# Two raw weight sums placed together on VectorE in the down-projection groups of a two-layer decoder trunk

## The chip, the cores and the metric

The kernel runs on one core of a Trainium2 chip. The metric is the device time of one execution in microseconds. A time before or after is the median over several runs; beside it stands one execution that was taken with the hardware profiler, and the rows of the trace come from that one.

## The reference

Two layers work on 512 tokens of width 1024, in float32. `ffn*_wd` is 2816 x 1024, `w_out` 1024 x 1024:

```python
for l in range(DEPTH):
    x = x + 0.5 * swiglu(rms_norm(x, ffn1_norm[l]), ffn1_wg[l], ffn1_wu[l], ffn1_wd[l])
    h = rms_norm(x, mix_norm[l])
    z = h @ w_in[l]                      # q, k, v and the three inputs of the convolution
    attn_out = sliding_window_attention(q, k, v, attn_sink[l])
    conv_out = short_conv(...)
    x = x + jnp.concatenate([attn_out, conv_out], axis=-1) @ w_out[l]
    x = x + 0.5 * swiglu(rms_norm(x, ffn2_norm[l]), ffn2_wg[l], ffn2_wu[l], ffn2_wd[l])
return rms_norm(x, final_norm)
# swiglu(h, g, u, d) = (silu(h @ g) * (h @ u)) @ d
```

## The kernel before

**Products in two parts.** Every operand of a matrix product is kept as a pair: a rounded high part and the rest. A weight tile is loaded as `raw` (128 x 1024 float32). ScalarE casts it to `wh` and VectorE subtracts, which gives `wl = raw - wh` (`split`, L226). TensorE multiplies three times: high by high, high by low, low by high.

**Seven products instead of eight.** Most of the large products are done in Strassen's manner, on two by two blocks. The weights then take seven forms (`FORMS`: a11, a12, s2, s3, s1, a22, s4) in this order. s1 and s3 are made while loading: SP's queue loads one block and POOL's queue adds another into the same tile (`need_raw`, L221). s2 is a11 + s1, summed on VectorE in place of a11 (L265). s4 is a12 + s2, which POOL's queue adds from tile to tile (L295). The products' accumulators are named x, y and w; `CHAINS` gives the order in which TensorE takes them. The activation forms are b11, b21, t2, t3, t1, t4 and b22, and they are split in the same way (`ft1h`, `ft1l` and so on).

**Groups.** The stages of a feed-forward network are written out by hand in `FIRST`, `INNER` and `LAST`. An entry ("s", b) is a group of down-projection products over 1024 of the 2816 inner columns. `plan` orders its weights with `seven`, and marks them "share": each form comes in two halves h = 0 and 1, so there are 14 weight tiles to a group. There are seven such groups: two in each of the first three networks, one in the last. In the first network the weights stand still and the activations stream in matmuls of 256 columns (`stand`, L815); in the others the matmuls have 512 columns (`stream`, L830). The output projection `w_out` uses the same forms, with `state["late"]` set.

**Order.** `take_split` hands TensorE its next weight pair and calls `need_split` for the pair two further on (`SPLIT_AHEAD` = 2). `need_split` calls `need_raw`, which issues loads at least four tiles ahead (`LOAD_AHEAD`). There are 8 places for raw tiles and 3 each for `wh` and `wl`. Apart from the opening and the end, a scheduler arranges each engine's instructions when the kernel is built, by dependences and priorities; `tc.issue_after(i)` makes what is inside come after the instruction i in this order. `state["rest"]` is the last split's subtraction. For a group "s" the sum of each half is issued after the last split's subtraction: so the first sum comes after a12's last subtraction, and the second sum after the subtraction of the first half of s2.

Of the kernel before, what the change touches and what calls it, by code (L numbers as in the profile page):

```python
# [75 lines left out]
def trunk_kernel(  # L76
# [23 lines left out]
    nc = tc.nc  # L100
# [94 lines left out]
    raw_of, split_of = {}, {}  # L195
    roomy = set()
    state = {"raw": 0, "split": 0, "group": 0, "late": None}
# [13 lines left out]
    def need_raw(u):  # L211

        while state["raw"] <= min(u, len(units) - 1):
            n = state["raw"]
            _, _, kc, _, wide = units[n][0]
            name, shape = f"raw_{n}", (P, kc, wide)
            r = form(name, F32, shape) if n in roomy else stock(name, shape=shape)
            if n >= OPEN:
                load(r, n, 0, kc)
            for more in units[n][1:]:  # L220
                nc.gpsimd.dma_start(out=r, in_=rows_of(*more), accum_op=ALU.add)  # L221
            raw_of[n] = r
            state["raw"] += 1

    def split(hi, lo, raw, eng=nc.vector):
        return nc.scalar.copy(hi, raw), eng.tensor_sub(lo, raw, f32(hi))  # L226

    def split_far(hi, lo, raw):

        nc.scalar.activation(lo, raw, AF.Copy, scale=-1.0)  # L230
        nc.scalar.copy(hi, raw)
        return nc.gpsimd.dma_start(out=f32(lo), in_=raw, accum_op=ALU.add)

    def need_split(g):
        while state["split"] <= min(g, len(order) - 1):
            n = state["split"]
            u, what = order[n]
            far = what == "far"
            if what in (None, "far"):
                need_raw(u if far else u + LOAD_AHEAD)  # L240
                raw = raw_of.pop(u)
            elif isinstance(what, tuple) and what[0] == "end":

                _, what, h = what
                at = {"a11": 2, "s2": 2, "s3": 3, "s1": 3, "a12": 4, "a22": 5, "s4": 5}[what]
                need_raw(u + 3 * at + h + LOAD_AHEAD)
                raws = {name: u + 3 * i + h for i, name in enumerate(END_LOADS)}
                if what == "s2":
                    with tc.issue_after(state["rest"]):
                        nc.vector.tensor_add(raw_of[raws["a11"]], raw_of[raws["a11"]], raw_of[raws["s1"]])  # L250
                raw = raw_of[raws["a11" if what in ("s2", "s4") else what]]
            elif isinstance(what, tuple):

                what, h, how = what
                far = how == "far"
                last = {"a11": 0, "a12": 4, "s2": 2, "s3": 6, "s1": 2, "a22": 8, "s4": 4}[what]
                need_raw(u + h if far else u + max(last, 4) + h + LOAD_AHEAD)
                a11, s1, a12, s3, a22 = (raw_of.get(u + 2 * i + h) for i in range(5))
                if what == "s2":

                    late = state["late"] if h else None
                    if not state["late"] and how == "share":
                        late = state["rest"]
                    with tc.issue_after(late) if late else nullcontext():
                        nc.vector.tensor_add(a11, a11, s1)  # L265
                raw = {"a11": a11, "a12": a12, "s2": a11, "s3": s3, "s1": s1, "a22": a22, "s4": a12}[what]
            else:

                need_raw(u + 4 + LOAD_AHEAD)
                a11, a12, s1, s3, a22 = (raw_of.get(u + i) for i in range(5))  # L270
                if what == "s2":
                    nc.vector.tensor_add(a11, a11, s1)
                if what == "s4":
                    nc.vector.tensor_add(a11, a11, a12)
                raw = {"a11": a11, "a12": a12, "s2": a11, "s3": s3, "s1": s1, "a22": a22, "s4": a11}[what]
                if what == FORMS[-1]:
                    for i in range(5):
                        del raw_of[u + i]
            shape = list(raw.shape)
            hi = wpool.tile(shape, F32R, tag="wh", bufs=3, name=f"wh_{n}")  # L280
            lo = wpool.tile(shape, F32R, tag="wl", bufs=3, name=f"wl_{n}")
            if far:
                sent = split_far(hi, lo, raw)
            else:
                state["cast"], state["rest"] = (i.ins for i in split(hi, lo, raw))
            if isinstance(order[n][1], tuple) and order[n][1][0] == "end":
                if what == "a12":
                    nc.gpsimd.dma_start(out=raw_of[raws["a11"]], in_=raw, accum_op=ALU.add)
                if what in ("s3", "s1", "a12", "a22"):
                    del raw_of[raws[what]]  # L290
                if what == "s4":
                    del raw_of[raws["a11"]]
            elif isinstance(order[n][1], tuple):
                if what == "s3" and how == "share":
                    nc.gpsimd.dma_start(out=a12, in_=a11, accum_op=ALU.add)  # L295
                elif what == "s3":
                    nc.vector.tensor_add(a12, a12, a11)
                done = {"s3": (0, 3), "s1": (1,), "a22": (4,), "s4": (2,)}.get(what, ())
                for i in done:
                    del raw_of[u + 2 * i + h]  # L300
            split_of[n] = (hi, lo)
            state["split"] += 1
            if far:

                with tc.issue_after(sent.ins):
                    need_raw(u + LOAD_AHEAD + (4 + h if isinstance(order[n][1], tuple) else 0))

    def take_split(ahead=SPLIT_AHEAD):
        n = state["group"]
        state["group"] += 1  # L310
        need_split(n + ahead)
        return n, *split_of.pop(n)
# [406 lines left out]
    with tc.manual_schedule(engines={pe, act, dve}):  # L719
# [41 lines left out]
        state["split"] = state["group"] = OPEN  # L761
        squares(2)
        need_split(OPEN)
        squares(3)

# [748 lines left out]
    def mix(l, norm, after):  # L1514
# [153 lines left out]
        def go_on():  # L1668

            nonlocal step  # L1670
            last = attend(step)
            step += 1
            with tc.issue_after(last.ins) if last else nullcontext():
                need_split(state["group"] - 1 + SPLIT_AHEAD)
# [89 lines left out]
```

## Time and profile before

| | us |
|---|---|
| median of 3 runs | 1645.42 |
| lowest and highest run | 1642.57, 1646.46 |
| profiled execution | 1643.27 |
| its span in the trace | 1641.5 |
| TensorE, matmul | 1631.8 busy |
| VectorE | 1376.5 busy |
| ScalarE | 1115.8 busy |
| GpSimd | 212.2 busy |

The granted TensorE clock was 0.999. A row of the timeline gives the start in us, the length in us, the engine, the line of the kernel, the operation, the tiles written and read, and a count; in brackets stands the idle time of the engine just before, and what ended it. The starts of two matmuls tell more than their lengths, since matmuls are pipelined. L815 and L830 are the products of `stand` and `stream`, L226 is `split`, L265 the sums, L221 and L295 the adding loads and copies of POOL's queue.

### The profile page before, as it was taken

The numbers are of one execution on the slowest core, as the hardware profiler recorded it, in microseconds if no ns is written. First come the engines' busy times: TensorE is split into PE (matmuls) and PEld (weight loads), VectorE is DVE, ScalarE is ACT, GpSimd is POOL, SyncE is SP. The second block draws the span as 40 slices with busy tenths as digits, with TensorE's granted clock in tenths as the row PEclk, the third lists the DMA queues.
The fourth block names the chain that finished last, engine by engine and source line by source line (L and its number), as shares of the span: only waits on it lengthen the run. The fifth ranks groups of instructions, "written<-read, shape, count | busy, mean of one in ns | idle before, by whom it ended". The sixth has DMA issues, their size and how long they took to land.

```text
span 1641.5 us, 22019 instructions
## 1 busy us (share of the span) xinstructions
PE 1631.8 (99%) x8060; PEld 1378.9 (84%) x8060; DVE 1376.5 (84%) x1812; ACT 1115.8 (68%) x1461; POOL 212.2 (13%) x188
## 2 busy tenths in 40 slices
PE   9999999999999999999999999999999999999998
PEld 7888889988898888888888888888888988888887
DVE  7987779987899977798998777989788998777997
ACT  6447776466567577777865777788565766777665
POOL 0011111100221011111011111110012111111121
PEclk9999999999999999999999999999999999999999
DMA  8379897741397689999966999999125967999992
GB/s 257 86 197 213 220 246 187 173 131 52 103 225 184 178 214 217 218 209 242 233 145 169 228 214 226 209 239 215 51 65 136 233 146 187 222 222 225 244 252 72
DMA packets 281504, 307.15 MB, mean 187 GB/s; under 512 B 98028, under 2 KB 166708, under 8 KB 281396
## 3 DMA queue, kind: packets, MB, share of 16 engines
q1 hardware_dynamic: 240804, 223.29, 47.2%
q0 software_dynamic: 39872, 81.80, 29.2%
q8 instruction: 63, 1.03, 0.2%
q10 hardware_dynamic: 720, 0.66, 0.1%
q14 instruction: 45, 0.37, 0.1%
HBM read 262.71 MB, written 2.10 MB: 161 GB/s over the span
## 4 chain that ended last, share of the span: by engine, by line
PE 93%; DVE 4%; ACT 1%; DMA 1%; issue 1%; SPq 0%; ACTq 0%; DVEq 0%
PE x L830 25%; PE y L830 13%; PE acc L324 7%; PE acc L325 7%; PE acc L327 7%; PE w L830 6%; PE x_s L830 5%; PE y_s L830 3%; PE x_m L815 3%; PE x_s L815 2%; PE w_s L830 2%; PE y_s L815 1%; PE y_m L815 1%; DVE wl L226 1%; PE acc L710 1%; PE x_e L830 1%
## 5 line engine op out<-in xcount | busy, mean ns | idle before, releaser
L226 ACT CAST wh<-raw 128x1024 fp32r<-128x1024 f32 (+1 forms) x491 | 511.1, 1044 | 363.0 <-PE x L830 91.9
L226 DVE TENSOR_TENSOR wl<-raw,wh 128x1024 fp32r<-128x1024 f32 (+1 forms) x491 | 594.8, 1218 | 175.3 <-ACT wh L226 174.0
L325 PE MATMUL acc<-xl,wh 128*128 128x512 f32 x424 | 165.7, 391 | 0.3 <-DVE xl L480 0.3
L324 PE MATMUL acc<-xh,wh 128*128 128x512 f32 x424 | 165.8, 392 | 0.0
L327 PE MATMUL acc<-xh,wl 128*128 128x512 f32 x416 | 162.3, 390 | 0.0
L221 POOL DMA_DIRECT2D raw<-in_ffn_wu_dram x39 | 49.0, 1256 | 394.6 <-DMA raw<-in_ffn_wu_dram 261.1
L325 PEld LDWEIGHTS acc<-xl,wh 128*128 128x128 f32 x424 | 79.7, 188 | 16.9 <-DVE xl L480 1.1
L324 PEld LDWEIGHTS acc<-xh,wh 128*128 128x128 f32 x424 | 79.8, 188 | 15.7
L327 PEld LDWEIGHTS acc<-xh,wl 128*128 128x128 f32 x416 | 78.1, 188 | 16.2
L221 POOL DMA_DIRECT2D raw<-in_ffn_wg_dram x39 | 48.1, 1258 | 228.6 <-DMA raw<-in_ffn_wu_dram 96.0
L221 POOL DMA_DIRECT2D raw<-in_ffn_wd_dram x34 | 41.0, 1209 | 249.0 <-DMA raw<-in_ffn_wd_dram 102.9
L265 DVE TENSOR_TENSOR raw<-raw,raw 128x1024 f32<-128x1024 f32 x56 | 68.0, 1219 | 3.9 <-DMA raw<-in_ffn_wu_dram 2.1
L1161 ACT COPY raw_a<-turned 128x1024 uint16<-128x1024 uint16 x48 | 63.1, 1355 | 0.0
L830 PE MATMUL w<-wh,fb21h 128*128 128x512 f32 x152 | 59.2, 390 | 0.0
L830 PE MATMUL x<-wh,ft2h 128*128 128x512 f32 x152 | 59.2, 390 | 0.0
L830 PE MATMUL y<-wh,ft3h 128*128 128x512 f32 x152 | 59.2, 390 | 0.0
L830 PE MATMUL x<-wl,ft1h 128*128 128x512 f32 x152 | 59.2, 389 | 0.0
L830 PE MATMUL x<-wh,ft1h 128*128 128x512 f32 x152 | 59.1, 389 | 0.0
L830 PE MATMUL w<-wh,fb21l 128*128 128x512 f32 x152 | 59.1, 389 | 0.0
L830 PE MATMUL x<-wl,ft2h 128*128 128x512 f32 x152 | 59.1, 389 | 0.0
L830 PE MATMUL w<-wl,fb21h 128*128 128x512 f32 x152 | 59.1, 389 | 0.0
L830 PE MATMUL x<-wh,ft2l 128*128 128x512 f32 x152 | 59.1, 389 | 0.0
(607 smaller groups left out, 4627.2 us busy)
## 6 DMA issues: line engine op xcount, KB each, us to landing
raw<-in_ffn_wu_dram SPq DMA_DIRECT2D x126, 512.0 KB, 5.4
raw<-in_ffn_wd_dram SPq DMA_DIRECT2D x105, 512.0 KB, 5.8
raw<-in_ffn_wg_dram SPq DMA_DIRECT2D x86, 512.0 KB, 5.3
raw<-in_ffn_wu_dram POOLq DMA_DIRECT2D x39, 512.0 KB, 9.1
raw<-in_ffn_wg_dram POOLq DMA_DIRECT2D x39, 512.0 KB, 6.6
raw<-in_w_in_dram SPq DMA_DIRECT2D x36, 512.0 KB, 3.8
raw<-in_ffn_wd_dram POOLq DMA_DIRECT2D x34, 512.0 KB, 9.5
raw<-raw POOLq DMA_DIRECT2D x21, 512.0 KB, 6.8
```

The costliest lines, as they stand in the source:

```text
L221: nc.gpsimd.dma_start(out=r, in_=rows_of(*more), accum_op=ALU.add)
L226: return nc.scalar.copy(hi, raw), eng.tensor_sub(lo, raw, f32(hi))
L265: nc.vector.tensor_add(a11, a11, s1)
L324: nc.tensor.matmul(acc, hi[:, k, :], rhs[k][0], start=k == first, stop=False)
L325: nc.tensor.matmul(acc, hi[:, k, :], rhs[k][1], start=False, stop=False)
L327: nc.tensor.matmul(acc, lo[:, k, :], rhs[k][0], start=False, stop=k == last)
L710: nc.tensor.matmul(opening[n], (lo if part == "w" else hi)[:, k, :], xl if part == "x" else xh, start=n not in begun, stop=k == KC - 1 and ...
L815: nc.tensor.matmul(accs[c // 2][:, c % 2, :], w[:, k, cols], x_[:, 2 * h + k, :], start=start and c % 2 == 0 and h + k + i == 0, stop=h + ...
L830: nc.tensor.matmul(accs[u], x_[:, 2 * h + k, tok], w[:, k, :], start=start and h + k + i == 0, stop=h + k == 2 and i == 2, skip_group_chec ...
L1161: nc.scalar.copy(words(raws[self.b][:, c, :]), self.to[:, :, c, :])
```

## The change

For the groups marked "share" outside the output projection, the sum of s2 is now made for both halves at the half h = 0: two sums, one after the other, both issued after the last split's subtraction, which is then that of a12's second half. At h = 1 nothing is summed. The branch for all other users of these forms keeps its sum and, in the output projection, its `state["late"]`. The number of instructions is the same on every engine.

```diff
-                if what == "s2":
-
-                    late = state["late"] if h else None
-                    if not state["late"] and how == "share":
-                        late = state["rest"]
-                    with tc.issue_after(late) if late else nullcontext():
+                if what == "s2" and how == "share" and not state["late"]:
+
+
+                    if h == 0:
+                        with tc.issue_after(state["rest"]):
+                            for k in range(2):
+                                to = raw_of[u + k]
+                                nc.vector.tensor_add(to, to, raw_of[u + 2 + k])
+                elif what == "s2":
+                    with tc.issue_after(state["late"]) if h and state["late"] else nullcontext():
                         nc.vector.tensor_add(a11, a11, s1)
```

In the order that the scheduler then writes, the two sums stand next to each other or with one subtraction or one update between them, ahead of the first `wl` of s2. In groups 1, 2, 4 and 6 TensorE's matmuls around s2 also change places among themselves. In the last group two loads of SP trade places with two of the closing stage.

## The prediction

> **What bounds the kernel now.** I read the page first: the busy times, the chain that ended last, and the group of the sums that the change moves.
>
> ```profile
> PE 1631.8 (99%) x8060; PEld 1378.9 (84%) x8060; DVE 1376.5 (84%) x1812; ACT 1115.8 (68%) x1461; POOL 212.2 (13%) x188
> PE 93%; DVE 4%; ACT 1%; DMA 1%; issue 1%; SPq 0%; ACTq 0%; DVEq 0%
> L265 DVE TENSOR_TENSOR raw<-raw,raw 128x1024 f32<-128x1024 f32 x56 | 68.0, 1219 | 3.9 <-DMA raw<-in_ffn_wu_dram 2.1
> ```
>
> TensorE (PE) is busy for 1631.8 of 1641.5 us and holds 93% of the chain. VectorE (DVE) is busy for 1376.5 us. So an edit on VectorE changes the time only where TensorE is seen to wait for it. A sum takes 1.22 us; 14 of the 56 are touched, two in each of seven groups "s", here numbered in order of time. No sum is added or removed: both are put before the first split, and the second no longer waits for it. Next I read the timeline of each group, VectorE, ScalarE (ACT) and TensorE in turn. Group 1:
>
> ```profile
> 258.41 1.22 DVE L265 TENSOR_TENSOR raw<-raw,raw 128x1024 f32<-128x1024 f32 x1
> 259.61 1.22 DVE L226 TENSOR_TENSOR ft1l_s<-raw_a,ft1h_s 128x1024 fp32r<-128x1024 f32 x1
> 260.82 1.23 DVE L226 TENSOR_TENSOR wl<-raw,wh 128x1024 fp32r<-128x1024 f32 x1
> 261.96 1.22 DVE L265 TENSOR_TENSOR raw<-raw,raw 128x1024 f32<-128x1024 f32 x1
> 264.37 1.23 DVE L226 TENSOR_TENSOR wl<-raw,wh 128x1024 fp32r<-128x1024 f32 x1 [1.19 <-ACT wh L226]
> ...
> 259.74 1.05 ACT L226 CAST wh<-raw 128x1024 fp32r<-128x1024 f32 x1 [0.16 <-DVE raw L265]
> 263.29 1.05 ACT L226 CAST wh<-raw 128x1024 fp32r<-128x1024 f32 x1 [2.50 <-DVE raw L265]
> ...
> 261.46 0.28 PE L815 MATMUL x_s<-ft2h_s,wh 128*128 128x256 f32 x1
> 261.58 0.28 PE L815 MATMUL x_s<-ft2l_s,wh 128*128 128x256 f32 x1
> 262.10 0.39 PE L815 MATMUL x_s<-ft2h_s,wl 128*128 128x256 f32 x1 [0.24 <-DVE wl L226]
> 265.34 0.39 PE L815 MATMUL y_s<-ft3h_s,wh 128*128 128x256 f32 x1
> 268.20 0.28 PE L815 MATMUL y_s<-ft3h_s,wl 128*128 128x256 f32 x1
> ```
>
> The old chain stands here: sum, cast on ScalarE, subtraction (wl), second sum, cast, subtraction, and VectorE is idle for 1.19 us before the last. TensorE's matmuls of 256 columns start 0.12 apart (261.46 to 261.58). So 262.10 is 0.40 late: it waits for the first wl, which ends at 260.82 + 1.23 = 262.05. And 265.34 is 0.26 late (the matmul before it starts at 264.96).
>
> Group 4 has the later form, with matmuls of 512 columns:
>
> ```profile
> 771.38 1.21 DVE L265 TENSOR_TENSOR raw<-raw,raw 128x1024 f32<-128x1024 f32 x1
> 772.51 1.22 DVE L226 TENSOR_TENSOR ft1l_s<-raw_a,ft1h_s 128x1024 fp32r<-128x1024 f32 x1
> 773.78 1.23 DVE L226 TENSOR_TENSOR wl<-raw,wh 128x1024 fp32r<-128x1024 f32 x1
> 774.93 1.22 DVE L265 TENSOR_TENSOR raw<-raw,raw 128x1024 f32<-128x1024 f32 x1
> 777.34 1.23 DVE L226 TENSOR_TENSOR wl<-raw,wh 128x1024 fp32r<-128x1024 f32 x1 [1.19 <-ACT wh L226]
> 780.70 1.23 DVE L226 TENSOR_TENSOR wl<-raw,wh 128x1024 fp32r<-128x1024 f32 x1 [0.94 <-ACT wh L226]
> ...
> 776.25 1.05 ACT L226 CAST wh<-raw 128x1024 fp32r<-128x1024 f32 x1 [2.50 <-DVE raw L265]
> ...
> 775.00 0.39 PE L830 MATMUL x_s<-wh,ft2h_s 128*128 128x512 f32 x1
> 778.17 0.39 PE L830 MATMUL x_s<-wh,ft2h_s 128*128 128x512 f32 x1
> 778.62 0.50 PE L830 MATMUL x_s<-wl,ft2h_s 128*128 128x512 f32 x1
> 778.95 0.39 PE L830 MATMUL x_s<-wh,ft2h_s 128*128 128x512 f32 x1
> 781.53 0.40 PE L830 MATMUL y_s<-wh,ft3l_s 128*128 128x512 f32 x1
> 781.99 0.50 PE L830 MATMUL y_s<-wl,ft3h_s 128*128 128x512 f32 x1
> ```
>
> 775.00 to 778.17 are 14 starts, so a pitch of 0.226. 778.62 comes 0.22 late for the second wl, and the start after it (778.95) is 0.10 slow as well: a stall of 0.33 us. 781.99 is late by 0.23 for the wl of 780.70, with the same tail: again 0.33. Group 6 is group 4's twin in the next layer and shows the pair in its row of 1101.77, below. The rest have cover, that is, the first wl is done well before TensorE first reads it:
>
> ```profile
> 1101.33 0.39 PE L830 MATMUL x_s<-wh,ft2h_s 128*128 128x512 f32 x1
> 1101.77 0.50 PE L830 MATMUL x_s<-wl,ft2h_s 128*128 128x512 f32 x1
> ...
> 312.04 1.22 DVE L226 TENSOR_TENSOR wl<-raw,wh 128x1024 fp32r<-128x1024 f32 x1
> 313.82 0.28 PE L815 MATMUL x_s<-ft2h_s,wl 128*128 128x256 f32 x1
> ...
> 734.19 1.23 DVE L226 TENSOR_TENSOR wl<-raw,wh 128x1024 fp32r<-128x1024 f32 x1 [1.36 <-ACT wh L226]
> 737.37 0.39 PE L830 MATMUL x_s<-wl,ft2h_s 128*128 128x512 f32 x1
> ...
> 1545.70 1.23 DVE L226 TENSOR_TENSOR wl<-raw,wh 128x1024 fp32r<-128x1024 f32 x1 [1.19 <-ACT wh L226]
> 1548.75 0.39 PE L830 MATMUL x_s<-wl,ft2h_s 128*128 128x512 f32 x1
> ```
>
> **The change part by part.** The profiled execution took 1643.27 us, 1.77 beyond its span; the median shown is 1645.42, 2.15 more. I sum against the former and carry the difference to the median. A step of VectorE starts 1.14 after the one before it when nothing is awaited (260.82 to 261.96). In the built order the sums come before the first wl, in groups 1, 4 and 6 with the subtraction ft1l beside them.
>
> Groups 3, 5, 7: the second sum falls into the idle 1.36 or 1.19 us in which VectorE waited for the first cast, so the first wl is not later. The second half's cast and wl come about 2 us earlier, and nobody waits for them: 737.37 and 1548.75 had 2 us of cover on the first half already. Cost 0. Group 2: the order puts sum, sum, wl ahead of two other subtractions, the first wl is earlier than 312.04 and had 0.6 us of cover. Cost 0.
>
> Group 1: sums at 258.41 and 259.55, ft1l at 260.69, first wl at 261.83 to 263.05. It comes 1.0 later, where TensorE already waited. The built order also lets TensorE take three y heads of the next weight but one before its first x with wl. Their cast is third on ScalarE: 259.74, then after the second sum's end (260.77) plus 0.11 (263.29 less 263.18) at 260.88, then 0.95 later at 261.83, done at 262.88. So y starts at 262.93, two more at about 263.15 and 263.27, and x with wl at 263.39. Then 20 and 24 matmuls at 0.12 give 268.67, where the same point (y with wl) was 268.20: plus 0.47. Bounds: minus 0.66, if both old stalls went, and plus 1.3, the delay of 262.10 with nothing saved behind it; I take the worked value, nearest to the rows.
>
> Groups 4 and 6: first wl at 774.79, done at 776.02. TensorE's new order runs four matmuls on wh first, so wl is needed at 775.00 + 4 x 0.226 = 775.90 and comes at 776.07: a stall of 0.17 and its tail 0.10. Second cast at 774.98 instead of 776.25, so second wl ends at 777.26, needed at 775.27 + 14 x 0.226 = 778.4: the stall of 0.33 goes. What follows on ScalarE moves up by up to 1.27, and the wl of 780.70 ends near 780.7, needed at about 781.7 (781.76 less what was gained): the other 0.33 goes too. Minus 0.39 each; bounds minus 0.66 and plus 0.5.
>
> What the second sum waits for: its source, a raw tile that the POOL queue adds into. It now stands at VectorE's head earlier, with the first wl behind it, and TensorE behind that. The tightest is group 4:
>
> ```profile
> 759.92 1.21 POOL L221 DMA_DIRECT2D raw<-in_ffn_wd_dram  x1 [4.38 <-DVE apart L897]
> ...
> raw<-in_ffn_wd_dram POOLq DMA_DIRECT2D x1, 512.0 KB, 10.0
> ```
>
> The second row is the DMA view's median from issue to landing in that one issue: landed near 771.1 at the latest, the sum would start at 773.65. No wait; the margin is 2.5 us. POOL keeps its order; its second copy of a sum into a12 can go 1.3 (group 4) to 2.4 us (group 1) earlier with the sum, and a12 is read last of the seven products. A load into the place that this copy frees (an a22 or the next a11, two loads of SP that trade places) is then sooner, not later. SP's order changes in group 7 alone: the first load for the closing stage goes behind two of the group, which wait for the copies.
>
> ```profile
> 1541.10 0.38 SPq L209 DMA_DIRECT2D raw<-in_ffn_wd_dram  x1
> ...
> 1573.46 1.22 DVE L226 TENSOR_TENSOR wl<-raw,wh 128x1024 fp32r<-128x1024 f32 x1
> ```
>
> The first row is that load, the second the wl made from it, 32 us later. Even 20 us later it would stand 12 ahead, and the POOL load shown above took 10.0: cost 0. Without that cover TensorE would wait once for the rest of it.
>
> Sum: 0.47 - 2 x 0.39 = -0.31. Profiled 1643.0, and against the median 1645.1 us.
>
> The Trainium skill (VectorE: DVE Perf Modes, The DRAIN you can't avoid) says that the next operation does not start until the pipeline is empty. The rows above have starts 1.14 apart for a length of 1.22, so they differ; by the rule each inserted sum would delay the first wl by 0.09 more in groups 1, 4 and 6, and the sum would be about -0.05.
>
> **The rivals.** *VectorE's idle time was on the path (faster).* The idle stretches before the wl come to about 1.2 in each group; were TensorE held by them seven times, 7 x 1.2 = 8.4 us go: 1637. For it: they are the longest idle of VectorE there. Against it: the visible waits of TensorE in these groups sum to 0.66 + 0.66 + 0.66 = 2.0 us. The Trainium skill (Perfetto Trace Analysis, Identifying the Most-Contended Engine) judges TensorE by its weight loads, not by its busy share. Those are 84% here, which would leave it idle room; but matmul starts at an even pitch between the waits leave none.
>
> *The first wl starves TensorE in all seven groups (slower).* It is one step of 1.14 us later wherever the idle stretch does not take the sum in; at 7 x 1.14 = 8.0 us that is 1653.4. It decides where the first wl is due less than 1.14 after its end. The rows give that for groups 1, 4 and 6 only; a second sum blocked by a late raw tile (over 2.5 us) would bring the others in.
>
> *Nothing moves:* the pair is only reordered within cover, 0 and 1645.4; it differs from the forecast by less than can be measured.
>
> **How the numbers follow.** A measurement here tells about 0.2%, 3.3 us, from no change: the three runs lie 3.9 us apart. Forecast 0.58, nothing moves 0.12, slower rival 0.20, faster rival 0.10. The first two are "same": 0.70. The forecast's own range is the bounds of its terms (-2.0 to +2.3) with half the runs' spread (1.9): 1641.5 to 1649.6. The lower half of the slower rival (three groups of seven starved, 3.4 us, and the spread) lies inside its upper end; left out are its upper half and the faster rival, 0.2. Range 1641.5 to 1649.5.
>
> **What would show it.** Right: the sums in pairs 1.14 apart; no 1.19 before the second wl; in group 1 TensorE's first x with wl near 263.4; no stall in group 4's y; groups 2, 3, 5, 7 unchanged. Wrong: a sum waiting for a DMA, a TensorE wait for wl over 0.3 us in group 3, 5 or 7, or the seven groups together changed by over 3 us.

## The result, and the profile after

The change made the kernel slower. The median after is 1652.74 us (7 runs, 1647.60 to 1657.63) against 1645.05 (7 runs) for before beside it, a ratio of 1.0054 (95% interval 1.0041 to 1.0068). Measured a second time it is 1647.77 (12 runs, 1645.32 to 1656.62) against 1643.24, a ratio of 1.0030 (1.0015 to 1.0045). The forecast was 1645.1 with a range of 1641.5 to 1649.5: the first median lies 3.2 us above the range, the second inside it. Either way the sign is wrong: the loss is 4.5 to 7.7 us and none was expected.

The page of after, the lines that answer to those of before (span, busy times, the chain that ended last):

```profile
span 1651.0 us, 22034 instructions
PE 1635.0 (99%) x8060; PEld 1380.6 (84%) x8060; DVE 1377.2 (83%) x1812; ACT 1116.4 (68%) x1461; POOL 212.4 (13%) x188
PE 89%; DVE 5%; ACT 2%; DMA 2%; issue 1%; SPq 0%; ACTq 0%; DVEq 0%
PE x L834 25%; PE y L834 13%; PE acc L329 7%; PE acc L328 7%; PE acc L331 6%; PE w L834 6%; PE x_s L834 5%; PE x_m L819 3%; PE y_s L834 3%; PE w_s L834 2%; DVE wl L226 2%; PE x_s L819 2%; PE y_m L819 1%; DMA turned<-halves 1%; PE y_s L819 1%
```

The busy times are those of before within 0.3%; the span is 9.5 us longer (the profiled execution took 1652.74). The chain has lost 4 points of TensorE, and one entry stands in its line now that did not before: the transposing DMAs `turned<-halves`, which belong to neither the sums nor the groups. (Lines behind the change are 4 higher than in before: L226 stays, L265 is L266, L295 is L299, L830 is L834.)

First the groups, as the prediction wanted them read. The timeline of after, VectorE and TensorE in groups 1, 4 and 6:

```profile
258.97 2.35 DVE L266 TENSOR_TENSOR raw<-raw,raw 128x1024 f32<-128x1024 f32 x2
263.48 0.39 PE L819 MATMUL y_s<-ft3h_s,wh 128*128 128x256 f32 x1 [1.06 <-ACT wh L226]
298.32 0.47 PE L328 MATMUL acc<-ah,wh 128*128 128x512 f32 x1 [0.55 <-DVE x L1329]
...
773.20 1.22 DVE L266 TENSOR_TENSOR raw<-raw,raw 128x1024 f32<-128x1024 f32 x1
774.33 1.22 DVE L226 TENSOR_TENSOR ft1l_s<-raw_a,ft1h_s 128x1024 fp32r<-128x1024 f32 x1
775.46 1.22 DVE L266 TENSOR_TENSOR raw<-raw,raw 128x1024 f32<-128x1024 f32 x1
776.60 2.51 DVE L226 TENSOR_TENSOR wl<-raw,wh 128x1024 fp32r<-128x1024 f32 x2
777.87 0.50 PE L834 MATMUL x_s<-wl,ft2h_s 128*128 128x512 f32 x1
1105.14 0.50 PE L834 MATMUL x_s<-wl,ft2h_s 128*128 128x512 f32 x1 [0.78 <-DVE wl L226]
```

Both kernels run the same 8060 matmuls, in the same order except close to groups 1, 2, 4 and 6. So the lag of after can be read from one and the same matmul in the two traces (start in us):

| matmul | before | after | lag |
|---|---|---|---|
| ahead of group 1's sums | 255.10 | 255.66 | 0.56 |
| behind group 1 | 282.00 | 283.02 | 1.02 |
| behind the wait near 298 | 305.06 | 306.88 | 1.82 |
| ahead of group 4's sums | 773.18 | 775.00 | 1.82 |
| behind group 4 | 790.07 | 791.42 | 1.35 |
| behind the first end (below) | 840.17 | 845.35 | 5.18 |
| ahead of group 6's sums | 1094.07 | 1099.22 | 5.15 |
| behind group 6 | 1108.00 | 1113.44 | 5.44 |
| behind the second end | 1170.00 | 1179.48 | 9.48 |
| behind group 7 | 1600.11 | 1609.62 | 9.51 |

The groups do about what was worked out. Group 1 costs 0.46 where 0.47 was forecast. In group 4 the two sums and the ft1l between them start 1.13 apart, the first wl ends at 777.82 and TensorE starts on it at 777.87; the group gains 0.47 where 0.39 was forecast. Group 6 waits 0.78 in one place and loses 0.29. Groups 2, 3, 5 and 7 change nothing (no more than 0.03 each).

The wait of 0.55 near 298, which costs 0.8, is no group's sum. Behind group 1 the scheduler has put the addition into `raw_a`, L613 in before and L617 in after, ahead of four additions of `acc` to x instead of behind them. VectorE, first before and then after:

```profile
295.70 2.48 DVE L1325 SCALAR_TENSOR_TENSOR x<-acc,x 128x512 f32<-128x512 f32 x4
300.43 1.21 DVE L613 TENSOR_TENSOR raw_a<-raw_a 128x1024 f32<-128x1024 f32 x1
...
290.62 1.22 DVE L617 TENSOR_TENSOR raw_a<-raw_a 128x1024 f32<-128x1024 f32 x1
297.49 2.48 DVE L1329 SCALAR_TENSOR_TENSOR x<-acc,x 128x512 f32<-128x512 f32 x4
```

The four come 1.79 later, TensorE was only 1.02 behind, and it waits for them.

Most of the 9.5 us are lost elsewhere: at the ends of the two networks whose last group is 4 or 6, 3.8 us at the first end and 4.0 at the second. There the products `acc` close the network (`down`, L1329 adds them to x), and the earlier parts of x come back from the transposes (`send` L908 on SP's queue, `back` L921 on ScalarE, L925 on VectorE). Then x is split into xh and xl (L483, L484) for the next stage, whose matmuls wait for it. The first of the two ends, in before:

```profile
779.28 4.17 SPq L209 DMA_DIRECT2D raw<-in_ffn_wd_dram  x4
783.55 3.10 SPq L904 DMA_TRANSPOSE turned<-halves  x1
782.48 1.99 ACT L141 COPY halves<-apart 128x1024 uint16<-128x1024 uint16 x2
...
802.99 0.39 PE L324 MATMUL acc<-ah,wh 128*128 128x512 f32 x1
805.12 5.02 ACT L917 COPY back<-turned 128x1024 uint16<-128x1024 uint16 x4
812.52 0.75 DVE L480 SCALAR_TENSOR_TENSOR xl<-x,par,xh 128x512 fp32r<-128x512 f32 x1
829.10 0.75 DVE L480 SCALAR_TENSOR_TENSOR xl<-x,par,xh 128x512 fp32r<-128x512 f32 x1
```

and in after, with the second end's waits last:

```profile
782.34 4.94 SPq L209 DMA_DIRECT2D raw<-in_ffn_wd_dram  x4
787.37 3.09 SPq L908 DMA_TRANSPOSE turned<-halves  x1
782.08 1.04 ACT L141 COPY halves<-apart 128x1024 uint16<-128x1024 uint16 x1
...
804.34 0.39 PE L328 MATMUL acc<-ah,wh 128*128 128x512 f32 x1
811.73 2.56 ACT L921 COPY back<-turned 128x1024 uint16<-128x1024 uint16 x2 [0.83 <-DMA turned<-halves]
818.15 0.75 DVE L484 SCALAR_TENSOR_TENSOR xl<-x,par,xh 128x512 fp32r<-128x512 f32 x1 [0.19 <-ACT xh L483]
833.27 0.75 DVE L484 SCALAR_TENSOR_TENSOR xl<-x,par,xh 128x512 fp32r<-128x512 f32 x1
...
832.81 0.50 PE L329 MATMUL acc<-xl,wh 128*128 128x512 f32 x1 [1.14 <-DVE xl L484]
834.07 0.78 PE L329 MATMUL acc<-xl,wh 128*128 128x512 f32 x1 [0.30 <-DVE xl L484]
1159.93 0.50 PE L328 MATMUL acc<-xh,wh 128*128 128x512 f32 x1 [1.15 <-ACT xh L483]
1161.57 0.62 PE L329 MATMUL acc<-xl,wh 128*128 128x512 f32 x1 [1.14 <-DVE xl L484]
```

Read each against the first matmul of the closing products (802.99 and 804.34), so that what was lost earlier drops out. SP's four loads start at -23.7 in before and -22.0 in after, the first transpose at -19.4 and -17.0; the last back copy ends at +7.2 and +9.9; the first xl starts at +9.5 and +13.8; the last at +26.1 and +28.9. TensorE had no wait at this end in before and has two in after, and at the second end 1.15 and 1.14 where before had 0.29 once. The first transpose reads `halves`. ScalarE finishes it at -19.5 in before (the first of the row's two) and already at -21.2 in after (782.08 + 1.04): in before the transpose starts when its input is ready, in after it stands behind the loads for 4.2 us. The windows of after give the price (busy time of each engine, then the granted TensorE clock):

```profile
832.00:834.60 2.60, 1.49 (x4) 0.97 (x5) 2.60 (x5) 0.78 (x2) 0.00 (x0) 0.91 0.53 128
834.60:837.60 3.00, 3.00 (x9) 2.31 (x7) 1.94 (x3) 2.85 (x3) 0.00 (x0) 0.51 0.17 64
...
1159.00:1161.60 2.60, 0.53 (x2) 0.22 (x2) 2.60 (x5) 2.38 (x4) 0.00 (x0) 1.00 0.07 21
1161.60:1165.10 3.50, 3.50 (x8) 2.44 (x9) 2.56 (x5) 1.67 (x3) 0.00 (x0) 0.53 0.57 154
```

TensorE idles 1.4 us at the first end (the two waits) and 2.3 at the second, and right after both its clock is about half. By the windows that is worth 0.09 x 2.60 + 0.49 x 3.00 = 1.7 us at the first end and 0.47 x 3.50 = 1.6 at the second. Waits and clock, less before's 0.29, are 6.8 of the 7.9 us that the two ends cost; the other 1.1 are not split up here.

### The profile page after: what moved, and what is told of

It is laid out like the page before. It is cut to its first block, busy times and chain, and to the rows that moved or that the text cites. A ratio compares the mean times of both kernels' runs of the same rounds, so it can differ in the third digit from the quotient of the medians.

```text
span 1651.0 us, 22034 instructions
## 1 busy us (share of the span) xinstructions
PE 1635.0 (99%) x8060; PEld 1380.6 (84%) x8060; DVE 1377.2 (83%) x1812; ACT 1116.4 (68%) x1461; POOL 212.4 (13%) x188
## 4 chain that ended last, share of the span: by engine, by line
PE 89%; DVE 5%; ACT 2%; DMA 2%; issue 1%; SPq 0%; ACTq 0%; DVEq 0%
PE x L834 25%; PE y L834 13%; PE acc L329 7%; PE acc L328 7%; PE acc L331 6%; PE w L834 6%; PE x_s L834 5%; PE x_m L819 3%; PE y_s L834 3%; PE w_s L834 2%; DVE wl L226 2%; PE x_s L819 2%; PE y_m L819 1%; DMA turned<-halves 1%; PE y_s L819 1%
## 5 line engine op out<-in xcount | busy, mean ns | idle before, releaser
L226 ACT CAST wh<-raw 128x1024 fp32r<-128x1024 f32 (+1 forms) x491 | 512.1, 1045 | 367.1 <-PE x L834 91.8
L226 DVE TENSOR_TENSOR wl<-raw,wh 128x1024 fp32r<-128x1024 f32 (+1 forms) x491 | 595.8, 1219 | 178.2 <-ACT wh L226 176.8
L834 PE MATMUL w<-wh,fb21h 128*128 128x512 f32 x152 | 59.2, 390 | 0.0
L834 PE MATMUL x<-wh,ft2h 128*128 128x512 f32 x152 | 59.2, 390 | 0.0
L834 PE MATMUL y<-wh,ft3h 128*128 128x512 f32 x152 | 59.2, 390 | 0.0
L834 PE MATMUL x<-wl,ft1h 128*128 128x512 f32 x152 | 59.1, 389 | 0.0
L834 PE MATMUL w<-wl,fb21h 128*128 128x512 f32 x152 | 59.1, 389 | 0.0
L834 PE MATMUL x<-wl,ft2h 128*128 128x512 f32 x152 | 59.1, 389 | 0.0
L834 PE MATMUL w<-wh,fb21l 128*128 128x512 f32 x152 | 59.1, 389 | 0.0
L834 PE MATMUL x<-wh,ft2l 128*128 128x512 f32 x152 | 59.1, 389 | 0.0
L834 PE MATMUL y<-wh,ft3l 128*128 128x512 f32 x152 | 59.1, 389 | 0.0
L834 PE MATMUL x<-wl,fb11h 128*128 128x512 f32 x152 | 59.1, 389 | 0.0
```

The lines of the kernel that those rows point to most:

```text
L834: nc.tensor.matmul(accs[u], x_[:, 2 * h + k, tok], w[:, k, :], start=start and h + k + i == 0, stop=h + k == 2 and i == 2, skip_group_chec ...
```

## The experiments

Four theories are told apart. **Q**, the queue: the copies land late, SP's loads that need their places hold up the transposes. **O**, the order: moving the sums also made the scheduler write another order for VectorE at the two ends. **W**, the recorded rival: the first wl starves TensorE in every group. **M**, margins: Q and O each eat a part of the same reserve, and only both together exceed it.

**Where does the loss sit?** `pair_4_6` and `pair_others` number the groups and take the new branch for some, the old one for the rest; the old branch is as before. Against after:

```diff
+    if what == "s2" and how == "share" and not state["late"] and h == 0:
+        state["seen"] = state.get("seen", 0) + 1
-    if what == "s2" and how == "share" and not state["late"]:
+    if what == "s2" and how == "share" and not state["late"] and state["seen"] in (4, 6):   # or: not in (4, 6)
```

> The two sums stand together in groups 4 and 6 only; the other five groups are as before. Theory Q (queue): the copies of groups 4 and 6 land together and late, four loads of SP that wait for their places hold up the transposes behind them, and TensorE waits at the two network ends near 833 and 1160 us: plus 6.5 to 8, about 1652. Theory O (order): the sums' move also changes the order of VectorE's closing additions and ScalarE's casts at those two ends, and that alone makes TensorE wait: also plus 6.5 to 8. Theory W (the recorded rival, first wl late in all groups): only two of seven groups pay, plus 2, about 1647.

> The two sums stand together in groups 1, 2, 3, 5 and 7 only; groups 4 and 6 are as before. Theories Q and O: plus 0.5 (group 1's worked cost), at most plus 1.5 with the two small waits near 298 and 445 us, about 1646. Theory W: five of seven groups pay, plus 5 to 6, about 1651.

Measured against before at 1643.40: `pair_4_6` 1644.96, ratio 1.0020 (1.0009 to 1.0030); `pair_others` 1645.78, ratio 1.0013 (1.0003 to 1.0022). A ratio here and below is not the quotient of the two medians, and the comparisons rest on the ratio and its interval. The first is smaller than Q and O said, the second by its median somewhat larger; W's 2 for the first comes near, its 5 to 6 for the second does not. The ten runs of `pair_4_6` fall in two heaps, six from 1643.95 to 1644.99 and four from 1648.57 to 1650.04. So these groups and their ends do not cost a fixed sum: the profiled execution, one of the six, has 0.77 us of waits at the first end and none at the second.

**Is it SP's queue?** `after_pool_loads` and its control `before_pool_loads` put the four loads (twice) on POOL's queue behind the copies.

```diff
-        nc.sync.dma_start(r[:, a:b, :], rows_of(src, k0 + a, b - a, col, wide))
+        queue = nc.gpsimd if n in pooled else nc.sync
+        queue.dma_start(r[:, a:b, :], rows_of(src, k0 + a, b - a, col, wide))
...
+                    if b == 5 and stages is INNER:
+                        pooled.update(range(len(units) + 8, len(units) + 12))
```

> The kernel after, with four loads in each of groups 4 and 6 (the two a22 halves and the first two tiles of the closing products, whose places the copies free) put on POOL's queue behind the copies instead of SP's; every other engine's order is the one of the kernel after. Theory Q: SP no longer waits for the copies ahead of the transposes, the first transpose of group 4 starts about 4 us earlier (near 783 instead of 787), the back additions are on time, and 6 to 8 of the loss come back: about 1646. Theory O: the order is unchanged, so the time stays at about 1652 to 1653. Theory W: stays at 1652.

> The kernel before with the same eight loads on POOL's queue: the control for the run with the kernel after. Theory Q: in the trace before the first transpose already started when its cast was done (783.55), so nothing is gained: 1645, within 1.5. Theories O and W: the same, 1645.

Measured: `after_pool_loads` 1646.25, ratio 1.0017 (1.0008 to 1.0026), as Q expected; its first transpose of the first end starts at 783.36 instead of 787.37, and TensorE has no wait there, though it still waits 1.42 us at the second end. But the control is a miss: `before_pool_loads` is slower, 1648.19, ratio 1.0026 (1.0013 to 1.0040). Its first transpose stays where it was (-19.4), yet the last back copy ends 1.7 us later at the first end and 2.0 at the second. So these loads on POOL have a price of their own, and the pair proves little. The next edit leaves them on SP.

**The order, and the queue without a side effect.** Four runs with before at 1643.24. `after_again` is after. `after_old_close` chains VectorE's instructions at the two ends in before's order, `before_new_close` chains them in after's; apart from the lines shown, no engine's order changes. A is the addition of `acc` to x, B that of `back`, W the wl of the next weights, X an xl, N the sum of squares:

```
before, after_old_close:  A5 B3 B2 W0 X4 A6 X5 N5 X6 N6 A7 W1 X7 N7 A0 A1 W2 X0 N0 X1 N1 A2 A3 W3 X2 N2 X3 N3
after, before_new_close:  B3 A5 W0 B2 A6 X4 X5 N5 X6 N6 A7 W1 X7 N7 A0 A1 W2 X0 N0 X1 N1 A2 A3 W3 X2 N2 X3 N3
```

```diff
+                for first, later in zip(names, names[1:]):
+                    behind(line[later], line[first])
```

`behind` sets an edge of issue order without a wait. The first x that is needed again, of B2, is added one wl and one addition later in after. In the traces, A5, B3 and B2, W0 of before, then B3, A5, W0, B2 of after:

```profile
809.55 0.68 DVE L1325 SCALAR_TENSOR_TENSOR x<-acc,x 128x512 f32<-128x512 f32 x1
810.17 1.29 DVE L921 TENSOR_TENSOR x<-x,back 128x512 f32<-128x512 f32 x2
811.38 1.22 DVE L226 TENSOR_TENSOR wl<-raw,wh 128x1024 fp32r<-128x1024 f32 x1
...
814.33 0.69 DVE L925 TENSOR_TENSOR x<-x,back 128x512 f32<-128x512 f32 x1 [1.50 <-ACT back L921]
814.93 0.68 DVE L1329 SCALAR_TENSOR_TENSOR x<-acc,x 128x512 f32<-128x512 f32 x1
815.53 1.22 DVE L226 TENSOR_TENSOR wl<-raw,wh 128x1024 fp32r<-128x1024 f32 x1
816.67 0.68 DVE L925 TENSOR_TENSOR x<-x,back 128x512 f32<-128x512 f32 x1
```

`after_sp_first` puts two transposes ahead of three of SP's waiting loads:

```diff
+                sent = nc.sync.dma_start_transpose(
...
+                if (o, t, u) == (0, 0, 1):
+                    for n in held.pop(0):        # units 9, 10 and 11 of the group
+                        behind(loads[n], sent)
```

> The kernel after once more, beside runs of before on the same chip, as the base of the other three. Theories Q and O: 1650 to 1653, with TensorE waits over 1 us at one or both network ends (near 833 and 1160 us) in the profile, and a granted clock below 0.999 in more than half of the runs. If it comes to about 1646.5 (the sum of the two part changes' medians over before, 1.6 + 2.4), the two parts add up and the first measurement lay high.

> The kernel after, with VectorE's order in the closing stage of the first two closing networks (after groups 4 and 6) put back to the one of before: the additions of x from acc and back stand before the wl of the next weight again; nothing else moves on any engine. Theory O: the last xl of the stage comes about 2 us earlier against TensorE's first matmul of the stage, from 28.9 to 27 in the first of the two, the waits shrink below 0.5 each, the clock stays at 0.999 and the time falls to about 1646.5. Theory Q: the transposes still start as late, so the time stays at 1650 or above, at most 1 us gained.

> The kernel after, with the first two transposes of each of these two networks put ahead of three of the four loads on SP's queue that wait for the copies; nothing else moves on any engine. Theory Q: the first transpose starts near 783 instead of 787, the back copies on ScalarE start without a wait for the transposes, the last xl comes 2 us earlier, and the time falls to about 1646.5. Theory O: the order on VectorE is unchanged and the time stays at 1650 to 1653.

> The kernel before, with VectorE's order in these two closing stages changed to the one of after and nothing else. Theory O: the last xl comes about 2 us later (26.1 to 28 against the stage's first matmul), TensorE waits over 1 us, and the time rises to 1648 to 1651. Theory Q: the transposes are on time, so the later order has slack: within 1 us of before.

| | median us | ratio to before | interval |
|---|---|---|---|
| after_again | 1647.77 | 1.0030 | 1.0015 to 1.0045 |
| after_old_close | 1644.70 | 1.0004 | 0.9993 to 1.0016 |
| after_sp_first | 1646.17 | 1.0014 | 1.0003 to 1.0025 |
| before_new_close | 1644.75 | 1.0006 | 0.9993 to 1.0018 |

`after_again` came out lower than expected, close to the sum of the two part changes. Of the 3.0 in a thousand, the order's repair takes away 2.6 and the queue's 1.6; the intervals of these two runs touch that of `after_again` or overlap it, so the sizes are rough. The order alone costs before little. Neither Q nor O explains all four: O fails on `before_new_close`, Q on `after_old_close`. M does.

The profiles show why. In all 32 closing stages profiled (16 profiles, two each), the first xl starts 2.37 to 2.39 us after the end of the last back copy with the old order, and 3.84 to 3.86 with the new one: the order costs the first xl 1.47 each time. Above: 812.52 less 810.14 in before, 818.15 less 814.29 in after. The last xl starts at 26.1 at the earliest with either order, so where the back copies end early enough (by 7.2 in these stages) the order costs nothing. And TensorE waits in all 18 stages whose last xl starts 27.2 us or later after the stage's first matmul, and in none of the 14 where it is 27.0 or less:

| stage | last back copy ends | last xl starts | TensorE's waits, sum |
|---|---|---|---|
| before, first end | 7.2 | 26.1 | 0 |
| before, second end | 9.9 | 27.5 | 0.29 |
| pair_4_6, first end | 9.1 | 28.0 | 0.77 |
| after_sp_first, first end | 8.9 | 27.9 | 0.59 |
| after_old_close, first end | 12.0 | 29.6 | 2.04 |
| before_new_close, second end | 11.0 | 30.0 | 2.16 |
| after, first end | 9.9 | 28.9 | 1.44 |
| after, second end | 11.5 | 30.5 | 2.29 |

The reserve is what TensorE still has to multiply at the end: before has 0.9 of it at one end and is 0.5 beyond it at the other. The profiled executions of `after_old_close` (1651.46) and `before_new_close` (1653.71) were the longest of their twelve runs: in both the transposes start late and TensorE waits at both ends. They do not stand for their medians. In `before_new_close` the lag behind before is 4.65 us already ahead of group 4's sums, and in the profile of `before_copies_close` further below it is 5.53: TensorE waits 1.91 and 2.64 us near 756 us, in group 3, ahead of the first instruction that either edit moves. POOL's two copies of group 3 took 10.3 and 13.3 us there, and 12.4 and 15.4, against 8.3 and 8.3 in before. Seven of the profiled kernels run the same instructions in the same order up to that point, and in these seven the two copies took from 5.7 to 15.4 us. So a copy can land late without any edit, and one profile does not tell the versions apart; that is for the medians and ratios.

**Do the other groups cost anything, and do the repairs add?** Four more runs, before at 1643.17. `pair_2357` takes the new branch in these groups only; `after_both` has both repairs; `not1_both` also leaves group 1 as before (`state["seen"] != 1`); `before_sp_first` is before with the two transposes first.

> The two sums stand together in groups 2, 3, 5 and 7 only, the four that the prediction costed at nothing. Theory M (margins: the loss is group 1's wait with its followers near 298 and 445 us, about 1.4, and the two closing stages after groups 4 and 6, about 4): within 0.7 us of before, about 1643.5, and no TensorE wait near 263 or 298 beyond those of before. Theory W (every group pays for the first wl, 1.14 each): plus 3 to 4.5, about 1647.

> The kernel after with both repairs: VectorE's closing order of before, and the first two transposes ahead of three loads on SP's queue. Theory M: the closing stages are as early as in before or earlier, what is left is group 1's 1.4 less up to 0.8 gained in groups 4 and 6: about 1644.2, as after_old_close or up to 1 less, with fewer runs over 1647. Theory W: still plus 3 or more, 1646.5.

> The same with group 1 left as in before: the sums stand together in groups 2 to 7. Theory M: nothing is left of the loss, 1642.8 to 1643.8, at or just under before; if the first wl's waits in groups 4 and 6 come at times (1.2 and 0.9 in two profiles), up to 1 more. Theory W: plus 3, 1646.

> The kernel before with the first two transposes of each closing network ahead of three loads on SP's queue, nothing else. Theory M: in before the transposes wait for nothing on SP that ends later than their cast, so the median stays at 1643.2 within 0.7; the runs in which TensorE waits at the network ends (over 1645, a third of them) may become fewer. If the loads that are put back come late for their casts, plus 1 to 2.

Measured: `pair_2357` 1644.82, ratio 1.0003 (0.9988 to 1.0018), `after_both` 1643.61, 0.9998 (0.9989 to 1.0007), `not1_both` 1643.32, 0.9997 (0.9987 to 1.0006), `before_sp_first` 1642.98, 0.9994 (0.9986 to 1.0003). The median of `pair_2357` is 1.65 above before, more than the 0.7 that M allowed; by the ratio it is 0.5. W is out: four groups with paired sums show no cost beyond the interval, where W had 3 to 4.5 us, and in the profile of `pair_2357` the only wait of TensorE of 0.2 us or more behind the opening is before's own 0.24 near 262. With both repairs the loss is back within the interval, although all fourteen sums stand where after has them. What stays is group 1: in the seven profiles whose group 1 has paired sums it costs 0.45 to 0.47, and what follows near 298 another 0.76 to 0.80. The wait near 298 is in each of the seven profiles whose group 1 has paired sums (0.50 to 0.55) and in none of `pair_4_6`, `pair_2357`, `not1_both`: it comes with group 1's new order. No run moves the addition into `raw_a` alone. The start of `after_both`'s first end, SP's queue:

```profile
784.02 0.37 SPq L210 DMA_DIRECT2D raw<-in_ffn_wd_dram  x1
784.48 4.21 SPq L955 DMA_TRANSPOSE turned<-halves  x2
788.79 1.59 SPq L210 DMA_DIRECT2D raw<-in_ffn_wd_dram  x3
```

One load, two transposes in 4.21 us, then the other three: the pair no longer waits for the second copy. No version here beats before by more than its interval; `before_sp_first` and `not1_both` come nearest.

**Is it enough without moving a sum?** `before_copies_together` holds POOL's first copy in groups 4 and 6 until the second sum is made; `before_copies_close` adds after's order on VectorE. Before was at 1643.12.

```diff
+                    if h == 0 and u in pairs:
+                        held = nc.gpsimd.tensor_copy(seen, raw_of[u + 1][:, 0, 0:1])
+                    with tc.issue_after(held.ins) if held else nullcontext():
                         nc.gpsimd.dma_start(out=a12, in_=a11, accum_op=ALU.add)
```

> The kernel before, with POOL's first copy in groups 4 and 6 held until the second sum is made (a one-element read of the second half on POOL ahead of it), so that both copies are issued back to back as in the kernel after; nothing else moves. This holds the first copy 3 us longer than after does. Theory P (the copies issued together land late, and SP's loads and the transposes behind them start late): the copies take 7 to 9 us each instead of 5 to 7, the first transpose of each closing network starts 2 to 3 us later, and alone, with the old order on VectorE, it costs 0 to 1.5: 1643.2 to 1644.7. Theory Q' (the copies' landing has nothing to do with it, the transposes are late in the kernel after for ScalarE's casts): the first transpose does not move, 1643.2.

> The kernel before with both: the two copies together in groups 4 and 6 as in the run beside it, and VectorE's closing order of the kernel after. No sum is moved. Theory P: these two together are the loss at the two network ends, and only together exceed what TensorE's lead covers: plus 2.5 to 4.5, about 1646.5, with waits over 1 us and a clock below 0.999 in a third or more of the runs. If the moved sums themselves (the later first wl) carry the loss: within 1.5 of before, as the run beside it and before_new_close.

Measured: `before_copies_together` 1646.46, ratio 1.0014 (1.0005 to 1.0023), `before_copies_close` 1651.51 (8 runs), ratio 1.0044 (1.0028 to 1.0061). The first is above the 1644.7 that theory P allowed at most, the second loses about twice what P expected; the other side, within 1.5 of before, is out. The order alone was 0.6 in a thousand, late copies alone 1.4, both 4.4: more than their sum, though the intervals (up to 1.8 and 2.3 alone, from 2.8 together) do not rule out plain addition. It is about as much as the change itself, 3.0 and 5.4, with every sum in its old place. So the two together suffice. They do not show that the sizes agree: at the first end of this profile SP's loads start at -20.5 and the first transpose at -15.9, 1.5 and 1.1 us later than in after. The waits of `before_copies_close` at the two ends are of the same kind as those of after:

```profile
782.65 1.79 POOL L333 DMA_DIRECT2D raw<-raw  x2 [0.72 <-issue]
788.02 4.56 SPq L210 DMA_DIRECT2D raw<-in_ffn_wd_dram  x4
792.67 3.18 SPq L947 DMA_TRANSPOSE turned<-halves  x1
816.61 2.56 ACT L960 COPY back<-turned 128x1024 uint16<-128x1024 uint16 x2 [1.12 <-DMA turned<-halves]
837.68 0.50 PE L363 MATMUL acc<-xl,wh 128*128 128x512 f32 x1 [1.14 <-DVE xl L522]
1165.79 0.50 PE L363 MATMUL acc<-xl,wh 128*128 128x512 f32 x1 [1.14 <-DVE xl L522]
```

One detail of theory P is half right: back to back, the first copy takes 4.5 to 5.3 us at the four ends of these two runs and the second 6.7 to 7.9, not both 7 to 9. In `before_copies_together` the first is late because it is held. In the profile of `before_copies_close`, the longest of its eight runs, the hold is not what sets the landing: POOL's last adding load lands late itself, and the copy 2.5 us behind it.

## Why the prediction was wrong

**The step that failed** is a term that the sum does not have. It adds up the groups and puts the closing stages after groups 4 and 6 at nothing; they cost 3.8 and 4.0 of the 9.5 us. Two of its steps lead there.

The first is on POOL and SP: "A load into the place that this copy frees ... is then sooner, not later." It took the copy's issue for its landing. The second copy of group 4 is indeed issued earlier (777.25 is 27.1 us ahead of the closing products, 776.71 was 26.3), but from issue to landing the two copies take 7.0 and 8.6 us, where before had 5.8 and 5.0. So SP's first load starts at 782.34, when the first copy lands (775.27 + 7.0), the second waits for the other copy (777.25 + 8.6), and the transposes come behind all four at 787.37. One profile alone would not show this, since landings vary, but the others agree: over the eight profiles with paired sums in groups 4 and 6 the second copy takes a median of 9.3 us in group 4 and 8.0 in group 6, over the six with these groups as in before and nothing held 6.4 and 6.0. The step priced the loads and did not ask what stands behind them on SP, though the next sentence of the prediction says of two loads in group 7 that they "wait for the copies". In after nothing shows that the loads themselves were missed; the transposes were.

The second is the reading of the built order, "the sums come before the first wl", which looks around the sums only. At the two closing stages, some 35 us behind the sums, B2 had moved behind A5 and W0. The price, 1.47 at the first xl, is one wl (1.14 by the rows of before) and part of an addition. The swap near 298 is a third place that this reading left out. The section on the change lists the new orders in the same way, around s2 alone.

The closing stages were never costed, since TensorE waited there for only 0.29 in before. That was taken for cover; it was all the reserve there is, 0.9 us at one end and less than none at the other. None of the signs of being wrong that the prediction names came up in after's trace, for they look at the groups alone.

**What was right.** Group 1's plus 0.47 (0.46 measured, and 0.45 to 0.47 in seven profiles) and the operations 1.14 apart; no sum waited for a DMA; groups 2, 3, 5 and 7 cost nothing that can be measured. **Mis-sized**: groups 4 and 6, at minus 0.39 each and at most plus 0.5. Group 4 gains 0.47 to 0.51 in five of the eight profiles with paired sums there, but loses 0.39 to 1.07 in three; group 6 gains 0.46 to 0.51 in six and loses 0.29 and 0.42 in two. In the losing ones the first wl comes late: TensorE waits 0.78 for it in after's group 6 and 1.05 in group 4 of `after_again`. The idle 1.19 us that the change removed was also VectorE's reserve for a late step ahead of it: in `after_again` VectorE comes to group 4's sums 2.3 us later than in before and TensorE only 1.1.

```profile
778.38 0.50 PE L834 MATMUL x_s<-wl,ft2h_s 128*128 128x512 f32 x1 [1.05 <-DVE wl L226]
```

**The rivals.** The slower rival had the right sign and, by 1653.4, even the first measurement's size, but the wrong mechanism: `pair_2357` shows no starved group. The Trainium skill (VectorE: DVE Perf Modes, The DRAIN you can't avoid) says that the next operation waits until the pipeline is empty, and by this the inserted sums would take 0.09 more each; but it says in the same place that an operation that is not held starts earlier. After's rows have starts 1.13 to 1.14 apart for lengths of 1.22 (773.20, 774.33, 775.46), which agrees with the latter. The 0.09 is no part of the loss.

**Why the copies land later.** The landing does not follow the copy's own issue. POOL's last adding load of group 4 is issued at 770.83 in before and lands 5.9 us later, at 776.7; in after it is 773.67 and 6.1, so 779.8. The first copy lands 2.5 us behind that in both, at 779.2 and 782.3, though it was issued 2.6 us behind the load in before and 1.6 in after. The same holds in 29 of the 32 cases (groups 4 and 6 of 16 profiles): 2.4 to 2.7 us from landing to landing, for issues 0.7 to 4.5 us apart; in group 3 it is 2.4 to 7.8. So a copy that is issued earlier behind the same adding load lands no earlier. Two of the other three are the copies that `before_copies_together` holds.

**What stays open.** Why the last adding load itself lands later in after, by 1.7 us in group 4 against the closing products, and why the second copy of group 4 follows the first by 3.5 us there and by 2.5 in before. Nor do the runs settle why the two measurements of after differ by 2.4 in a thousand.

## What to carry to other kernels

When an edit moves an instruction, compare the whole built order of every engine before costing it, to the end of the program: here one half of the loss was a swap that the scheduler made some 35 us further on. Cost a freed buffer by when the transfer that frees it lands, which can hang on what stands ahead of it on its queue, and follow the in-order queue of whoever waits for it to the last thing queued behind. And measure each stage's reserve (how much later the last input may come before TensorE waits), since two delays that are each inside it are free, and together are not.

## What the runs showed of the hardware

TensorE's granted clock fell to about half after waits that were short and not in one piece. In after it is 0.50 from 834.2 to 837.5 us, behind 1.44 us of waits, the longest of them 1.14, and 0.50 from 1161.9 to 1165.1, behind 2.29; shortly before and behind both stretches it is 1.00. It does not follow each time: of the twelve closing stages with 1.42 us of waits or more, matmul starts at twice the usual pitch follow in six, and not behind 1.98 in `before_pool_loads` nor 2.04 in `after_old_close`. The Trainium skill (TensorE: Matmul & The Clock Gate, Part 1: The HAM clock gate) has the clock halved after at least one idle window of about 3.4 us; no wait here is that long, so the trace shows the drop earlier than by that rule. The time at the lower clock, 3.4 us at the first end by the windows above (1.7 us lost at half clock), agrees with the page's warm-up window of about 3.4 us.

The loss is uneven between executions, and the clock goes with it: of the twelve runs of `after_again`, five have a mean clock of 0.999 and take 1645.3 to 1647.7 us, and the seven with 0.997 or 0.998 take 1646.6 to 1656.6. But one drop is worth 1.7 us, so the clock is only a part of this spread; the rest is not shown, since one execution of each kernel has a trace.

An adding copy of 512 KB on POOL's queue took from 4.4 to 15.4 us from issue to landing in the 16 profiles. Behind an adding load of the same size on that queue it landed 2.4 to 2.7 us after the load in 29 of the 32 cases of groups 4 and 6, for issues 0.7 to 4.5 us apart.
